# A SwiGLU layer as seven block products, and causal attention by pairs of heads, in a whole-model kernel

## The chip, the cores and the metric

The kernel runs on one core of a Trainium2 chip, as one launch that computes two transformer blocks. The metric is the device time in microseconds (us). The core has five engines with a queue each: TensorE (PE, matrix products; its weight loads are listed apart, as PEld), VectorE (DVE), ScalarE (ACT), GpSimd (POOL) and SyncE (SP, which issues most DMAs). Each engine works through its own queue in order, and an instruction starts when the results that it waits for are there.

## The reference, cut to what matters

The model has a first block (windowed attention and a spatial gate beside each other, then a mixture of experts) and a second block of two layers (a retention and state-space mixer in layer 0, a latent attention in layer 1), each layer followed by a SwiGLU feed-forward. All inputs are float32. The change touches two places.

The feed-forward of layer 1, on 512 tokens of 1024 features, with 2816 hidden features:

```python
def swiglu(h, w_gate, w_up, w_down):
    return (jax.nn.silu(h @ w_gate) * (h @ w_up)) @ w_down
...
h_lat = h_lat + m_lat[5] * swiglu(modulate(rms_norm(h_lat), m_lat[3], m_lat[4]),
                                  w_ffn_gate[i], w_ffn_up[i], w_ffn_down[i])
```

The first block's attention, 8 heads of 64 features on 512 tokens:

```python
DILATION_PATTERNS = ((128, 1), (512, 4), (2048, 16))
...
def dilated_mixture_attention(q, k, v):
    res = [dilated_window_attention(q, k, v, w, d) for (w, d) in DILATION_PATTERNS]
    m_all = jnp.stack([r[1] for r in res], 0)
    l_all = jnp.stack([r[2] for r in res], 0)
    o_all = jnp.stack([r[0] for r in res], 0)
    wts = l_all * jnp.exp(m_all - jnp.max(m_all, 0, keepdims=True))
    o = jnp.sum(wts[..., None] * o_all, 0) / jnp.sum(wts, 0)[..., None]
```

The three patterns weighted by their denominators are one causal softmax over all earlier keys, in which a key counts as often as patterns hold it. The kernel computes it so, with a table `amask` that is added to the scores.

## The kernel before, in words

The program is built by a scheduler that takes operations in the order in which the code gives them, with their tile pools, and writes out one queue per engine; within a queue nothing is reordered on the chip. A tile pool with a tag and `bufs=n` is a ring of n buffers: a new tile waits until the last reader of the one n tiles ago is done.

A float32 matrix product with full precision is three products of a shorter format: `split` (L238) makes of a tile a rounded part h (a cast on ACT, L239) and a rest l (a subtraction on DVE, L240), and `mm3` (L245) issues A_h B_h, A_h B_l and A_l B_h. Weights arrive by DMA in `wr` (a ring of 6 buffers of 128x1024), and their parts go to `wh` and `wl` (rings of 4).

The feed-forward of layer 1 is the class `FFN` with one sequence of 512 tokens; in this text it is the second feed-forward layer. Hidden features are taken in 11 chunks of 256, each of two blocks of 128 (`mi`). `gate_up(c)` makes for a block the gate product and the up product: 8 feature tiles x 3 matmuls of 512 columns each, into two PSUM tiles `gb`, 48 matmuls; then silu (ACT, L1490), the product with the up half (DVE, L1491) and the split of the result into `hidh` and `hidl`. Chunk 0 does it in halves of 256 columns (`cb`). `down(c)` multiplies the chunk's hidden features by two 128x512 tiles of down weights for each of four token tiles (`ob`, 48 matmuls of 512 columns, two PSUM banks "dn"), and DVE adds each `ob` to the accumulators `acc0` to `acc3` (L1534 for the first chunk, L1536 for the later). `run` gives out gate_up(c + 1) before down(c), for c up to 9; the scheduler then sets the 48 down products of chunks 0 to 8 between the gate products of the chunk two later, or next to it, as results come.

In the first block's attention a loop over 8 heads makes for each head four score products (one for each tile of 128 queries, against 128, 256, 384 or 512 keys; K = 64, so a head lies on rows 0 to 63 or 64 to 127), adds the mask and takes the maximum on DVE (L395, L396), the exponential on ACT, four reciprocals in one instruction, the scaling on DVE (L402), ten transposes on PE (`tpb`, L409), their copies, and for two heads together the value products (`pvb`). Between them `fill` sets products of the second block's conditioning (`adb`), FL[3] = 3 of them after each head.

## The time and profile before

| | before |
|---|---|
| device time, median of 3 runs | 2349.05 us (2348.92 to 2360.97) |
| the profiled execution | 2353.49 us, its span 2351.7 us |
| mean granted TensorE clock | 0.977 |
| PE busy | 2252.5 us, 96% |
| DVE, ACT, POOL busy | 61%, 34%, 19% |
| first block's attention | 86 to 156 us |
| feed-forward of layer 0 | 1005 to 1560 us |
| feed-forward of layer 1: chunk 0 | 1975 to 2001 us |
| feed-forward of layer 1: gate, up and down, chunks 1 on | 2001 to 2289 us, then the last down products |

Busy times are of one execution, taken by the profiler. They don't add up over engines, since engines work beside each other. A chain of waits is followed back from an instruction to what released it, so it shows which engine set the time at each moment; an engine with a high busy share that is not in the chain has time to spare. The granted clock is the share of TensorE's full clock that the chip gave it.

### The profile page before, as it was taken

Reading aid. Unit: us, or ns where it says so; the run is one execution under the profiler, and the core shown is the slowest. Engines: PE = TensorE matmul, PEld = TensorE weight load, DVE = VectorE, ACT = ScalarE, POOL = GpSimd, SP = SyncE. Lnnn points to the kernel's source line nnn. Section 1 sums busy time; section 2 is a strip of 40 time slices with the busy share of each in tenths; the row PEclk is TensorE's granted clock in tenths of the full one; section 3 lists DMA queues with packets and bytes.
Section 4 is the critical chain, followed back from the end, with each engine's and each line's share of the span. In section 5 each row is a group of like instructions: output and inputs, shape, how many; then the busy total and the mean of one; then the engine's idle time right before and its main releaser. Section 6 shows DMA issues by size and latency. Waiting matters only on the chain.

```text
span 2351.7 us, 30149 instructions
## 1 busy us (share of the span) xinstructions
PE 2252.5 (96%) x11748; PEld 1688.6 (72%) x11748; DVE 1423.6 (61%) x2341; ACT 794.9 (34%) x1382; POOL 442.9 (19%) x331
## 2 busy tenths in 40 slices
PE   9999999999979988899999999989999999999998
PEld 7667755534458756688888888877877668888876
DVE  8766743434475577776677753465568765444446
ACT  4344323222253243342211112134446545222222
POOL 0010310232250256410000000531022123000006
PEclk9999999999989997999999999999999999999999
DMA  8655498998853001344344331221100043332230
GB/s 297 217 183 202 182 373 332 371 389 336 310 197 99 30 28 54 125 152 135 122 139 135 126 108 55 65 97 62 60 1 1 1 147 107 106 99 92 87 106 39
DMA packets 99151, 338.91 MB, mean 144 GB/s; under 512 B 14373, under 2 KB 16293, under 8 KB 99002
## 3 DMA queue, kind: packets, MB, share of 16 engines
q1 hardware_dynamic: 94394, 324.33, 39.1%
q0 software_dynamic: 4608, 12.59, 1.5%
q8 instruction: 94, 1.54, 0.3%
q14 instruction: 55, 0.45, 0.1%
HBM read 323.21 MB, written 17.86 MB: 145 GB/s over the span
## 4 chain that ended last, share of the span: by engine, by line
PE 72%; DVE 8%; issue 3%; POOL 2%; ACT 2%; DMA 0%; POOLq 0%; SPq 0%; DVEq 0%; ACTq 0%
PE gb L243 22%; PE ob L243 14%; PE ga L243 10%; PE cb L243 6%; PE gu L243 5%; PE sc L243 3%; PE yb L243 3%; PE ptb L1808 2%; DVE wl L240 1%; POOL rs_r L290 1%; PE kb L243 1%; PE vb L243 1%; PE ntb L920 1%; PE ssd_x L243 1%; PE tpm L687 1%
## 5 line engine op out<-in xcount | busy, mean ns | idle before, releaser
L239 ACT CAST wh<-wr 128x1024 fp32r<-128x1024 f32 (+1 forms) x239 | 249.1, 1048 | 629.1 <-PE gb L243 274.9
L240 DVE TENSOR_TENSOR wl<-wr,wh 128x1024 fp32r<-128x1024 f32 (+1 forms) x235 | 309.2, 1323 | 216.4 <-ACT wh L239 211.8
L243 PE MATMUL gb<-fh,wh 128*128 128x512 f32 x672 | 264.0, 393 | 0.0
L243 PE MATMUL gb<-fh,wl 128*128 128x512 f32 x672 | 263.9, 393 | 0.0
L243 PE MATMUL gb<-fl,wh 128*128 128x512 f32 x672 | 263.7, 392 | 0.0
L243 PE MATMUL ob<-wh,hidh 128*128 128x512 f32 x440 | 173.9, 395 | 4.4 <-DVE gob L1529 3.0
L243 PE MATMUL ob<-wl,hidh 128*128 128x512 f32 x440 | 172.5, 392 | 0.0
L243 PE MATMUL ob<-wh,hidl 128*128 128x512 f32 x440 | 172.3, 392 | 0.0
L1536 DVE TENSOR_TENSOR acc<-acc,ob 128x512 f32<-128x512 f32 x160 | 108.3, 685 | 84.6 <-PE ob L243 84.6
L860 DVE SCALAR_TENSOR_TENSOR adacc<-wr,cond,adacc 128x512 f32<-128x512 f32 x224 | 152.9, 752 | 1.4 <-DMA wr<-in_w_ada 1.4
L243 PEld LDWEIGHTS gb<-fh,wl 128*128 128x128 f32 x672 | 126.2, 188 | 28.7
L243 PEld LDWEIGHTS gb<-fl,wh 128*128 128x128 f32 x672 | 126.2, 188 | 27.7
L243 PEld LDWEIGHTS gb<-fh,wh 128*128 128x128 f32 x672 | 126.2, 188 | 27.4
L243 PE MATMUL gu<-mw,xgT 128*64 128x512 f32 x512 | 124.3, 600 | 0.7 <-issue 0.7
L243 PE MATMUL cb<-fh,wh 128*128 128x256 f32 x416 | 118.0, 284 | 0.0
L243 PE MATMUL cb<-fl,wh 128*128 128x256 f32 x416 | 117.6, 283 | 0.0
L243 PE MATMUL cb<-fh,wl 128*128 128x256 f32 x416 | 117.0, 281 | 0.0
L1538 POOL TENSOR_TENSOR acc<-acc,gate 128x1024 f32<-128x1024 f32 x10 | 28.1, 2811 | 468.1 <-DVE acc L1536 468.1
L290 POOL TENSOR_TENSOR rs_r<-rs_v,mhalf 128x1 f32<-128x1 f32 (+1 forms) x54 | 46.4, 861 | 336.8 <-DVE rs_v L288 336.5
L243 PEld LDWEIGHTS ob<-wh,hidh 128*128 128x128 f32 x440 | 82.6, 188 | 24.8 <-DVE gob L1529 3.2
L1491 DVE TENSOR_TENSOR sg<-sg,gb 128x512 f32<-128x512 f32 x42 | 28.9, 688 | 112.3 <-PE gb L243 112.2
L243 PEld LDWEIGHTS ob<-wh,hidl 128*128 128x128 f32 x440 | 82.7, 188 | 18.3
(666 smaller groups left out, 4891.3 us busy)
## 6 DMA issues: line engine op xcount, KB each, us to landing
mw<-in_w_gu SPq DMA_DIRECT2D x128, 512.0 KB
wr<-in_w_ada SPq DMA_DIRECT2D x96, 512.0 KB
mw<-in_w_dn SPq DMA_DIRECT2D x64, 512.0 KB
wr<-in_w_fg SPq DMA_DIRECT2D x44, 512.0 KB
wr<-in_w_fu SPq DMA_DIRECT2D x44, 512.0 KB
wr<-in_w_fd SPq DMA_DIRECT2D x44, 512.0 KB
wr<-in_w_ret SPq DMA_DIRECT2D x28, 512.0 KB
wr<-in_w_in SPq DMA_DIRECT2D x19, 512.0 KB
```

The lines of the kernel that those rows point to most:

```text
L239: self.nc.scalar.copy(h, src)
L240: (eng or self.nc.vector).tensor_tensor(l, src, h.bitcast(F32), ALU.subtract)
L243: self.nc.tensor.matmul(out, lhsT, rhs, start=start, stop=stop, **kw)
L290: nc.gpsimd.tensor_tensor(r, v, self.mhalf[:, :n], ALU.pow)
L687: nc.tensor.transpose(bank[:, k, :], xg[:, (j * 4 + k) * P:(j * 4 + k + 1) * P], self.ident)
L860: V.scalar_tensor_tensor(acc[:, r], W[:, k], s, acc[:, r], op0=ALU.mult, op1=ALU.add)
L920: nc.tensor.transpose(bank[:, j, i * P:i * P + P], hp[i][:, (2 * kk + j) * P:(2 * kk + j + 1) * P], self.ident)
L1491: nc.vector.tensor_tensor(t, t, out[1], ALU.mult)
L1536: V.tensor_tensor(a[:, sl], a[:, sl], ob, ALU.add)
L1538: G.tensor_tensor(a, a, gate(tt), ALU.mult)
L1808: nc.tensor.transpose(bank[:, qt * P:qt * P + P], prs[h][qt][:, kt * P:kt * P + P], K.ident)
```

## The change

**Feed-forward of layer 1.** With `seven=True`, chunks 1 to 10 no longer compute the gate and the up half as two products. The activations (1024 features x 512 tokens) and the pair of weights are cut in 2 x 2 blocks (feature halves by token halves; gate and up by feature halves), and the 2 x 2 block product is formed by Winograd's variant of Strassen's scheme: seven products of blocks instead of eight, of sums of blocks, and sums of the seven. `sums` forms four sums of activation blocks once and splits them; `prep(m)` forms for each block of 128 hidden features four sums of weight blocks on POOL (L1510 to L1513) and splits gate, `sa`, `sb` and up; `seven_up(m)` issues the seven products (4 feature tiles x 3 matmuls x 256 columns each), two copies on ACT, five additions from PSUM on DVE, two additions on POOL (L1544, L1545), silu, and the product of the halves on DVE (L1549). `sa` and `sb` take places in the ring `wr`; `sah` and `sal` have rings of two in a new pool. The weights, the down products and the accumulators stay (the accumulator add is L1632 there).

**First block's attention.** The loop goes over four pairs of heads and the query tiles from the last to the first. The scores of the two heads of a pair are issued one behind the other, on rows 0 to 63 and rows 64 to 127, into banks of two tags; the softmax with its reciprocal is done for each head and query tile; transposes and value products of a pair are issued between the scores of the next. Fills are (2, 2, 1, 1) per pair.

```diff
-FL = (0, 1, 1, 3, 1)
+FL = (0, 1, 1, (2, 2, 1, 1), 1)
...
-        for h in range(8):
-            hp, b0 = h // 2, 64 * (h % 2)
...
-            for qt in range(NT):
-                n = (qt + 1) * P
-                sc = ps.tile([P, 512], F32, name="sc", tag="sc", bufs=2)
-                self.mm(sc[:, :n], qT[b0:b0 + 64, hp, qt * P:qt * P + P], kT[b0:b0 + 64, hp, :n], True, True)
...
-            V.reciprocal(ri, ls)
...
-            fill(FL[3])
+        room = self.res.rearrange("p t d -> p (t d)")[:, :2560].rearrange("p (i n) -> p i n", i=2)
+        def scores(p, qt):
+            n = (qt + 1) * P
+            sc = [ps.tile([P, 512], F32, name="sc", tag=tag, bufs=2) for tag in ("sc", "mm")]
+            for c in range(2):
+                r = slice(64 * c, 64 * c + 64)
+                self.mm(sc[c][:, :n], qT[r, p, qt * P:qt * P + P], kT[r, p, :n], True, True)
+            for c in range(2):
...
+                V.tensor_tensor(pv, sc[c][:, :n], amask[:, 512 - n:], ALU.add)
+                V.tensor_reduce(mx, pv, AX, ALU.max, negate=True)
+                S.activation(pv, pv, AF.Exp, bias=mx, accum_out=ls)
+                V.reciprocal(ls, ls)
+                V.tensor_scalar(pv, pv, ls, None, op0=ALU.mult)
...
+        for p in range(5):
+            for i in range(NT):
+                if p < 4:
+                    scores(p, NT - 1 - i)
+                    fill(FL[3][i])
+                if p and i:
+                    spread(p - 1, i - 1)
+                    if i > 1:
+                        values(p - 1, i - 2)
+            if p:
+                spread(p - 1, 3)
+                for jt in (2, 3):
+                    values(p - 1, jt)
...
+    def sums(self):
+        V, G = self.nc.vector, self.nc.gpsimd
+        (f11, f12), (f21, f22) = self.F
+        G.tensor_tensor(f11, f12, f11, ALU.subtract)
+        V.tensor_tensor(f12, f22, f12, ALU.subtract)
+        G.tensor_tensor(f22, f22, f11, ALU.subtract)
+        V.tensor_tensor(f21, f21, f22, ALU.subtract)
...
+        for n, t in (("t3", f12), ("t2", f22), ("t4", f21), ("t1", f11)):
...
+            self.K.split(t, h, l)
...
+    def prep(self, m):
...
+        g, u = (K.wraw(self.I[n][self.layer, m], (8, P)) for n in ("w_fg", "w_fu"))
+        sa, sb = K.w4("sa").rearrange("p (k c) -> p k c", c=P), K.w4("sb")[:, :512].rearrange("p (k c) -> p k c", c=P)
+        lo, hi = slice(0, 4), slice(4, 8)
+        G.tensor_tensor(sb, u[:, lo], u[:, hi], ALU.add)
+        G.tensor_tensor(sa[:, lo], sb, g[:, lo], ALU.subtract)
+        G.tensor_tensor(sa[:, hi], g[:, lo], u[:, lo], ALU.subtract)
+        G.tensor_tensor(u[:, lo], g[:, hi], sa[:, lo], ALU.subtract)
+        gs = K.wcut(g, (8, P))
+        sh, sl = (self.hpool.tile([P, 8, P], F32R, name=n, tag=n, bufs=2) for n in ("sah", "sal"))
+        K.split(sa, sh, sl)
+        ss = K.wcut(sb, (4, P))
+        us = K.wcut(u, (8, P))
...
+    def seven_up(self, m, hid, mi):
...
+        def product(a, t):
+            b = ps.tile([P, 512], F32, name="w" + a, tag="gu", bufs=6)[:, :w]
+            for k in range(4):
+                K.mm3(b, A[a](k), B[t](k), k == 0, k == 3)
+            return b
...
+        S.copy(c12, product("a11", "b11"))
+        V.tensor_tensor(c11, c12, product("a12", "b21"), ALU.add)
+        V.tensor_tensor(c12, c12, product("s2", "t2"), ALU.add)
+        V.tensor_tensor(c21, c12, product("s3", "t3"), ALU.add)
+        S.copy(m5, product("s1", "t1"))
+        self.prep(m + 1)
+        G.tensor_tensor(c12, c12, m5, ALU.add)
+        G.tensor_tensor(c22, c21, m5, ALU.add)
+        V.tensor_tensor(c12, c12, product("s4", "b22"), ALU.add)
+        V.tensor_tensor(c21, c21, product("a22", "t4"), ALU.add)
+        S.activation(t, t, AF.Silu)
+        V.tensor_tensor(t, t, v, ALU.mult)
+        K.split(t, hid[0][:, mi, :], hid[1][:, mi, :])
...
+        if self.seven and c:
+            for mi in range(2):
+                self.seven_up(2 * c + mi, hid, mi)
+            return hid
```

In the DVE queue of before, around the end of a chunk's second block, the two down-weight splits (`wl_17151` and `wl_17157`) stand in these rows, with the product of gate and up (L1491), the gate and up splits of the next block and the first accumulator add:

```order
L240 TENSOR_TENSOR wl_17151<-wr_17148,wh_17150 128x1024
L1491 TENSOR_TENSOR sg_17088<-sg_17088,gb_17039 128x512
L240 TENSOR_TENSOR wl_17157<-wr_17154,wh_17156 128x1024
L240 TENSOR_TENSOR hidl_17013<-sg_17088,hidh_17012 128x512
L240 TENSOR_TENSOR wl_17229<-wr_17226,wh_17228 128x1024
L1491 TENSOR_TENSOR sg_17143<-sg_17143,gb_17094 128x512
L240 TENSOR_TENSOR wl_17235<-wr_17232,wh_17234 128x1024
L240 TENSOR_TENSOR hidl_17013<-sg_17143,hidh_17012 128x512
L1536 TENSOR_TENSOR acc0_15917<-acc0_15917,ob_17160 128x512
L1536 TENSOR_TENSOR acc0_15917<-acc0_15917,ob_17168 128x512
```

The same place in the DVE queue of after; `wl_17988` and `wl_17994` are the down weights, L1541, L1546, L1547 and L1539 the sums out of PSUM, `sal` the rest of `sa`:

```order
L1541 TENSOR_TENSOR su_17853<-sg_17852,ws3_17897 128x256
L240 TENSOR_TENSOR wl_17948<-wr_17927,wh_17947 128x1024
L1546 TENSOR_TENSOR sg_17852<-sg_17852,ws4_17953 128x256
L1547 TENSOR_TENSOR su_17853<-su_17853,wa22_17967 128x256
L1549 TENSOR_TENSOR sg_17852<-sg_17852,su_17853 128x512
L240 TENSOR_TENSOR wl_17988<-wr_17985,wh_17987 128x1024
L240 TENSOR_TENSOR sal_18151<-sa_18140,sah_18150 128x1024
L240 TENSOR_TENSOR hidl_17718<-sg_17852,hidh_17717 128x512
L1632 TENSOR_TENSOR acc0_15977<-acc0_15977,ob_17997 128x512
L1539 TENSOR_TENSOR sg_18063<-sg_18063,wa12_18080 128x256
L240 TENSOR_TENSOR wl_17994<-wr_17991,wh_17993 128x1024
L1632 TENSOR_TENSOR acc0_15977<-acc0_15977,ob_18005 128x512
```

The first down weight's split now stands behind the product of the halves (L1549) and the second behind the first accumulator add, where both stood ahead of the block's last split before. The POOL queue of after has at this place, where that of before has nothing:

```order
L1510 TENSOR_TENSOR sb_18141<-wr_18138 128x512
L1544 TENSOR_TENSOR sg_17852<-sg_17852,m5_17854 128x256
L1545 TENSOR_TENSOR su_17853<-su_17853,m5_17854 128x256
L1511 TENSOR_TENSOR sa_18140<-sb_18141,wr_18136 128x512
L1512 TENSOR_TENSOR sa_18140<-wr_18136,wr_18138 128x512
L1513 TENSOR_TENSOR wr_18138<-wr_18136,sa_18140 128x512
L1510 TENSOR_TENSOR sb_18274<-wr_18271 128x512
```

The first weight sum of the next block (`sb`) stands ahead of the two sums of the current block, the other three (`sa` twice, `wr` for the changed up half) right behind them.

In the first block's attention the PE queue of before begins with one head's scores, with `adb` fills between:

```order
L243 MATMUL sc_835<-kT_781,qT_780 128x128
L243 MATMUL sc_840<-kT_781,qT_780 128x256
L243 MATMUL adb_328<-wr_890,cond_131 32x128
L243 MATMUL sc_845<-kT_781,qT_780 128x384
L243 MATMUL adb_328<-wr_890,cond_131 32x128 x2
L243 MATMUL sc_850<-kT_781,qT_780 128x512
L243 MATMUL adb_328<-wr_900,cond_131 32x128 x8
L243 MATMUL sc_913<-kT_781,qT_780 128x128
L243 MATMUL adb_328<-wr_969,cond_131 32x128 x5
L243 MATMUL sc_918<-kT_781,qT_780 128x256
L243 MATMUL sc_923<-kT_781,qT_780 128x384
```

In the queue of after, the second pair of heads has its scores of 512, 384 and 256 columns here, with fills and the first pair's transposes (`tpb`):

```order
L243 MATMUL sc_965<-kT_781,qT_780 128x512
L243 MATMUL adb_328<-wr_984,cond_131 32x128 x7
L243 MATMUL sc_966<-kT_781,qT_780 128x512
L243 MATMUL adb_328<-wr_984,cond_131 32x128
L243 MATMUL adb_328<-wr_994,cond_131 32x128 x8
L243 MATMUL sc_1004<-kT_781,qT_780 128x384
L243 MATMUL sc_1005<-kT_781,qT_780 128x384
L243 MATMUL sc_1067<-kT_781,qT_780 128x256
L415 MATMUL tpb_1054<-c_ident_63,pr_836 128x128 x4
L415 MATMUL tpb_1061<-c_ident_63,res_65 128x128 x4
L243 MATMUL sc_1068<-kT_781,qT_780 128x256
L415 MATMUL tpb_1095<-c_ident_63,pr_836 128x128 x3
```

The two scores of 384 columns are neighbours in the queue; those of 512 have fills between them, and those of 256 transposes.

## Rows read from the trace of the kernel before

**Rows 1.** The page, busy time of each engine.

```profile
PE 2252.5 (96%) x11748; PEld 1688.6 (72%) x11748; DVE 1423.6 (61%) x2341; ACT 794.9 (34%) x1382; POOL 442.9 (19%) x331
```

**Rows 2.** Windows: us, busy of each engine, granted clock, DMA share, GB/s.

```profile
2001.00:2289.00 288.00, 288.00 (x1259) 236.12 (x1259) 129.69 (x154) 75.44 (x91) 1.95 (x1) 1.00 0.30 97
...
85.00:156.00 71.00, 71.00 (x620) 39.64 (x620) 50.12 (x127) 38.87 (x100) 0.00 (x0) 1.00 0.59 200
```

**Rows 3.** Chain of waits, 2022.8 us on: start, us, engine, tile, line, count.

```profile
2022.79 2.80 PE ob L243 x12
2025.59 0.92 PE gb L243 x4
2026.51 8.39 PE ob L243 x36
2034.90 20.88 PE gb L243 x92
```

**Rows 4.** Chain of waits, chunk 0 of the second feed-forward layer.

```profile
1985.17 15.83 PE cb L243 x132
```

**Rows 5.** Groups, 2022.8 to 2088.8 us: shapes, count, busy us, mean ns, idle.

```profile
L240 DVE TENSOR_TENSOR wl<-wr,wh 128x1024 fp32r<-128x1024 f32 x12 | 14.7, 1224 | 14.2 <-ACT wh L239 13.7
...
L239 ACT CAST wh<-wr 128x1024 fp32r<-128x1024 f32 x13 | 13.7, 1053 | 53.0 <-PE gb L243 21.9 <-PE ob L243 19.4 <-issue 11.7
...
L1536 DVE TENSOR_TENSOR acc<-acc,ob 128x512 f32<-128x512 f32 x8 | 5.4, 684 | 4.0 <-PE ob L243 4.0
...
L240 DVE TENSOR_TENSOR hidl<-sg,hidh 128x512 fp32r<-128x512 f32 x4 | 2.7, 685 | 0.0
```

**Rows 6.** Timeline of 128x256 instructions: start, us, engine, line, operation, tiles.

```profile
1968.94 0.73 POOL L931 TENSOR_TENSOR fl<-ntf,fh 128x256 fp32r<-128x256 f32 x1 [4.42 <-ACT ntf L928]
...
1989.33 0.42 DVE L1491 TENSOR_TENSOR sg<-sg,cb 128x256 f32<-128x256 f32 x1 [1.85 <-ACT sg L1490]
```

**Rows 7.** Timeline, end of first feed-forward layer, POOL, DVE.

```profile
1548.35 5.08 POOL L1530 TENSOR_TENSOR res<-res,gob 128x512 f32<-128x512 f32 x4
...
1550.93 0.69 DVE L1529 TENSOR_TENSOR gob<-ob,gate 128x512 f32<-128x512 f32 x1 [0.67 <-POOL res L1530]
...
1553.01 0.96 DVE L1530 TENSOR_TENSOR res<-res,gob 128x512 f32<-128x512 f32 x1
```

**Rows 8.** Timeline around 161 us, POOL and DVE.

```profile
161.61 2.39 POOL L436 TENSOR_TENSOR wsp<-wsp,c_utri 128x1024 f32<-128x1024 f32 x1
...
161.69 2.87 DVE L447 TENSOR_TENSOR res<-res,ggb 128x512 f32<-128x512 f32 x1 [1.40 <-POOL res L446]
```

**Rows 9.** Timeline around 1974 us, DVE and POOL.

```profile
1974.20 2.35 DVE L240 TENSOR_TENSOR wl<-wr,wh 128x1024 fp32r<-128x1024 f32 x2
...
1974.35 2.80 POOL L931 TENSOR_TENSOR fl<-ntf,fh 128x256 fp32r<-128x256 f32 x1 [2.11 <-ACT ntf L928]
```

**Rows 10.** First block's attention: groups of matmuls, then timeline.

```profile
L243 PE MATMUL sc<-kT,qT 64*128 64x128 f32 (+3 forms) x64 | 22.8, 464 | 0.0
L243 PE MATMUL adb<-wr,cond 128*32 128x128 f32 x374 | 17.8, 279 | 0.0
L409 PE MATMUL tpb<-c_ident,pr 128*128 128x128 f32 x80 | 15.2, 292 | 0.0
L243 PE MATMUL pvb<-pt,v 128*64 128x256 f32 (+3 forms) x64 | 14.4, 447 | 0.0
...
90.52 0.48 PE L243 MATMUL sc<-kT,qT 64*128 64x128 f32 x2
...
93.33 1.12 PE L243 MATMUL sc<-kT,qT 64*128 64x512 f32 x2
...
94.73 0.33 PE L409 MATMUL tpb<-c_ident,pr 128*128 128x128 f32 x1
...
104.05 2.37 PE L243 MATMUL pvb<-pt,v 128*64 128x512 f32 x14
...
874.20 1.79 PE L243 MATMUL ret_s<-qT,kT 64*128 64x128 f32 x16
```

More of the change, by code (lines that the diff above doesn't have):

```diff
@@ L407, in block1, with spread @@
+        def spread(p, jt):
+            o, w = sum((NT - j) * P for j in range(jt)), (NT - jt) * P
+            for c in range(2):
+                if jt == 0:
+                    PTs[p, c] = p1.tile([P, 1280], F32, name="pt", tag="pt", bufs=3)
                 bank = ps.tile([P, 512], F32, name="tpb", tag="tp", bufs=2)
@@ L902, in rms, with norm_T @@
         return hn
-    def norm_T(self, hs, hn, nt, layer, which, row, outh, outl, pool, ps, tag, bufs):
+    def norm_T(self, hs, hn, nt, layer, which, row, outh, outl, pool, ps, tag, bufs, keep=None):
         nc = self.nc
@@ L925, in norm_T @@
                     nc.scalar.activation(h, bank[:, j, :], AF.Identity, scale=sc, bias=sh)
-                    f = pool.tile([P, 512], F32, name="ntf", tag="ntf", bufs=3)[:, :256]
+                    f = keep(k, pair) if keep else pool.tile([P, 512], F32, name="ntf", tag="ntf", bufs=3)[:, :256]
                     if j:
@@ L1418, with __init__ @@
 class FFN:
-    def __init__(self, K, layer, seqs, ps):
+    def __init__(self, K, layer, seqs, ps, seven=False):
+        self.seven = seven
+        self.preps = {}
         self.K, self.nc, self.I, self.layer, self.seqs, self.ps = K, K.nc, K.I, layer, seqs, ps
@@ L1435, in norm @@
         self.xs[si] = vh, vl, w
-        yield from self.K.norm_T(hs, hn, nt, self.layer, 1, row, vh, vl, npool, ps or self.ps, tag, bufs)
+        keep = None
+        if self.seven:
+            self.F = [[pool.tile([P, 4, 256], F32, name=f"xf{i}{j}", tag="xf", bufs=5) for j in range(2)] for i in range(2)]
+            keep = lambda k, pair: self.F[k // 4][pair][:, k % 4, :]
+        yield from self.K.norm_T(hs, hn, nt, self.layer, 1, row, vh, vl, npool, ps or self.ps, tag, bufs, keep)
     def open(self, pool):
-        self.pool = pool
+        self.pool = self.hpool = pool
         n = self.off[-1]
@@ new lines, in prep @@
+    def prep(self, m):
+        if m in self.preps or m >= DFF // P:
+            return
+        K, G = self.K, self.nc.gpsimd
+        g, u = (K.wraw(self.I[n][self.layer, m], (8, P)) for n in ("w_fg", "w_fu"))
[10 more added lines that the diff above has]
+        us = K.wcut(u, (8, P))
+        part = lambda t, o: lambda k: (t[0][:, o + k, :], t[1][:, o + k, :])
+        self.preps[m] = dict(a11=part(gs, 0), a12=part(gs, 4), s3=part((sh, sl), 4), s2=part((sh, sl), 0),
+                             s4=part(us, 0), a22=part(us, 4), s1=part(ss, 0))
@@ L1542, in run @@
         hid = self.gate_up(0)
+        if self.seven:
+            self.sums()
         for c in range(nch - 1):
@@ L2113, in body @@
         pg = opened("pg", k.pool("pg"))
-        f1 = FFN(k, 1, [(NT, 0)], psg)
+        f1 = FFN(k, 1, [(NT, 0)], psg, True)
         f1.open(pg)
```

69 lines of the change are left out of this document (35 added, 34 removed).

## The prediction

> **What bounds the kernel now.** I read the page first: TensorE (PE) is busy for 2252.5 of 2351.7 us, VectorE (DVE) for 61% of the span, ScalarE (ACT) for 34%, GpSimd (POOL) for 19% [rows 1]. The share is an average, so the windows come next, one on each place of the change. In the gate, up and down products of the second feed-forward layer (2001 to 2289 us) PE is busy in all 288.00 us, at a granted clock of 1.00, which is the 2.4 GHz level; DVE works 129.69 us there, and POOL does one instruction. In the first block's attention (85 to 156 us) PE is full too, DVE works 50.12 of 71 us and POOL nothing [rows 2]. The chain of waits through one period of the feed-forward (one chunk of 256 hidden columns) holds PE and nothing else: 12 down products, 4 gate products, 36 down products, 92 gate and up products, 2.80 + 0.92 + 8.39 + 20.88 = 32.99 us [rows 3]. So time can be won there only with fewer or cheaper products, and it is lost as soon as another engine delivers later than PE asks.
>
> **The seven products, PE.** Before, a block of 128 hidden columns took 48 matmuls of 512 columns (the chunk's 96 in [rows 3]); it now takes 7 x 4 x 3 = 84 of 256. A gate matmul of 512 takes 20.88/92 = 0.227 us [rows 3]; the nearest row for 256 is chunk 0 of the same layer, which the kernel before already does in halves: 15.83/132 = 0.120 us [rows 4]. So 84 x 0.120 - 48 x 0.227 = 10.08 - 10.90 = -0.82 us for a block, and -16.3 us for the 20 blocks of chunks 1 to 10. One eighth fewer columns give only 7.5%, since the step of a short matmul has a fixed part. By the ends: were 256 columns half of a 512 step (0.1135), 84 would cost 9.53 us and the 20 blocks win 27 us; that row's 0.120 has weight loads beside every matmul as the new products do, so I take it, and -20 (0.118, a rounding of it in 20 blocks) as the good end.
>
> **The seven products, the other engines.** Per block, with durations of [rows 5]: DVE had two splits of 128x1024 (1.22), one product (0.69) and one split (0.69), and now has three splits of 1024, one of 512, five sums out of PSUM of 128x256 (0.42 by [rows 6]), the product and its split: 3 x 1.22 + 0.69 + 5 x 0.42 + 2 x 0.69 = 7.8 us in place of 3.8. A chunk has two blocks, eight accumulator adds (0.68) and two splits of down weights: 15.6 + 5.5 + 2.4 = 23.5 us in a period of 168 x 0.120 + 48 x 0.2325 = 31.3 us on PE (0.2325 is 8.39/36). ACT has eight instructions per block and two casts per chunk, none over the 1.05 us of a cast of 1024: under 19 us in a period, which PE covers. POOL goes from nothing to four 128x512 sums (5.08/4 = 1.27 us each [rows 7]) and two of 128x256 (0.73 [rows 6]) per block, 13.2 us per period. Each engine alone fits below 31.3 us. The ring of six raw weights now also holds two sums per block, so weight transfers are issued later; the DMA engines are busy 0.30 of this stretch [rows 2], and I price that at nothing, up to 1 us per chunk if a landing is what PE waits for.
>
> They don't work alone. A DVE product of two SBUF operands, 0.69 us by itself, took 2.87 us when it started 0.08 us after a POOL instruction of 2.39 us: it stood until POOL was done [rows 8]. Beside the four POOL sums that ran from 1548.35 to 1553.43, a DVE instruction that reads PSUM took its normal 0.69 us, and one with both operands in SBUF 0.96 us, ending 0.5 us after POOL [rows 7]. It goes both ways: a POOL subtraction of 0.73 us took 2.80 us beside two DVE splits [rows 9]. All splits, the product of gate and up, and POOL's sums are of that kind; the PSUM sums and the accumulator adds aren't.
>
> That agrees with the Trainium skill, "SBUF — State Buffer", "Who interferes with whom": an exclusive lock, taken by whichever starts first and held for the whole instruction, between a DVE instruction with two SBUF inputs and a GpSimd instruction that reads SBUF. It speaks against this change, as nothing in the steady period of before used POOL: by it the stall worked out next is 3.2 us per chunk, and if both engines only went on side by side it would be 0.7. The 2.87 us agrees with it; the 0.96 us is a shorter wait than a whole POOL instruction would give.
>
> I walk one period by hand with the order of the changed kernel and these durations; t = 0 is the end of an odd block's last product. POOL has its two 256 sums (after the copy of m5, which ACT makes behind a weight cast) from -0.65 to 0.7, and then three 512 sums queued. The first holds 0.7 to 1.95. DVE's product of gate and up comes at 1.4, behind the silu, and waits to 1.9, ends 2.55. POOL's second holds 2.5 to 3.75. Next on DVE is the split of the first down weight: it waits to 3.7 and ends 4.85. PE asks for it at 2.62: after 12 gate products (1.44), one down product, which needs only the cast, and 8 more gate products comes the first down product that reads the split part. PE is in order, so it stands 2.3 us. POOL's third sum holds to 6.05, then DVE's split of sa to 7.15, the split of the hidden block 7.75, and the first accumulator add 8.35, where PE wanted its bank at 7.85: 0.5 to 0.6 more. The second down weight is split by 9.85, wanted at 9.6: 0.3 more. Together 3.2 us, in each of the 9 chunks whose down products are interleaved (0 to 8): +28.8 us. Behind the waiting splits stand the accumulator adds, and PE's two banks for down products wait for these. The same walk with DVE and POOL side by side leaves 0.7 us, since the split of the down weight stands behind the silu and the product in DVE's order either way: +6.3 over the 9 chunks. An upper end is an alternation over the whole period: 23.5 + 13.2 = 36.7 us against the 32.99 of before, which is +5.4 over PE's 31.3, 9 times +49.
>
> **The start.** The sums of activations and the first blocks' sums of weights are new work between the norm and chunk 1. Chunk 0 ends at 2001.0 on PE (1985.17 + 15.83, [rows 4]). From about 1987 DVE has two sums and four splits of 1024, the first block's four splits, the chunk's products and hidden splits: some 13 us; POOL has two 1024 sums (2.39 each) and seven 512 sums in that stretch: 14 us. In turn they need up to 27 us, side by side 14, and PE has 14 us of chunk 0 to cover them, then 10 us of block products that need only the first of them. I put +6.5 us, bounds 3 (side by side) and 10.
>
> **The attention.** It has 64 score matmul records (22.8 us), 374 fill products (17.8), 80 transposes (15.2), 64 value matmuls (14.4) [rows 10]. A score product of 512 columns (fp32, two records) takes 1.12 us by itself, one of 128 columns 0.48. Two heads on the two halves of the rows can share the array: the later stage with K = 64 does 16 records of 128 columns in 1.79 us, 0.11 each, where the two of 128 alone take 0.24 each [rows 10]. Of the 16 pairs only 9 stand back to back in the new order; 7 have a fill, a transpose or a value product between them. Half of 9/16 of 22.8 would be -6.4; I take -5.5, since short pairs also pay their start. The value products overlapped in pairs before (14 in 2.37 us); more of them are now split: +2.2. The first pair's softmax (two heads by four blocks on DVE, 32 reciprocals where 8 were) must end before the first transpose, which came at 94.73 us; I estimate 12.4 us from the first score, and fills that cover all but 1.8 us. Fills are 24 blocks as before. Sum -5.5 + 2.2 + 1.8 = -1.5, bounds -6 (all of the overlap, no idle) and +4 (none, idle 4). Elsewhere in the program a few instructions change places on every engine; I price that at nothing, 3 us to either side.
>
> **Sum.** -16.3 + 28.8 + 6.5 - 1.5 = +17.5 us on the profiled execution of 2353.49 us, which is 4.4 us over the median of the runs, 2349.05. So 2371 as a profile, **2366 us** as a median.
>
> **Rivals.**
> 1. Lock without loss: POOL's sums fall where DVE is in PSUM sums or idle, and PE stands 0.7 per chunk. -16.3 + 6.3 + 3 - 1.5 = -8.5: 2340 us; with 0.118 and the whole attention, 2329. For it: DVE has 7.8 us free per period; against: three POOL sums are queued just where the down weights are split. Chance 0.27.
> 2. Half: a stall of 2 us per chunk (one POOL sum less in the way, because after a stall of PE the splits come earlier relative to the products): -16.3 + 18 + 4 - 1.5 = +4: 2353 us. Chance 0.27.
> 3. DVE with POOL becomes the bound over the whole period: it decides when waiting in turn takes more than 31.3 us; DVE's 23.5 plus 13.2 is 36.7, less what DVE does meanwhile without the lock, 9.7 us of PSUM sums and accumulator adds. +5 per chunk in the worst case: -16.3 + 45 + 8 - 1.5 = +35: 2384 us. Against: four tenths of DVE's time are free of the lock. Chance 0.10.
> 4. The attention loses what it should win because split pairs step as single ones: +6 on any case; it lies inside the ranges.
> My forecast has 0.36.
>
> **Range and chances.** What a measurement here can tell from no change is about 0.5%, 11.7 us: faster is below 2337.3, slower above 2360.8. The forecast runs from 2356 to 2376 (stalls 2.1 to 4.3). Faster: two thirds of rival 1 and little else, 0.22. Slower: the forecast but for its low end, a fifth of rival 2, rival 3: 0.47. Same: 0.31. The range leaves out the good end of rival 1 and half of rival 3: 2334 to 2382.
>
> **What would show it.** In the profile of the changed kernel: products w... at 0.120 us each, 84 per block (else the first term). Idle of PE in front of down products, put down to DVE's split of a down weight, 2 to 3 us once per chunk, and DVE splits of 1024 that take 2 to 2.5 us beside a POOL sum (else the lock's term; with no such idle rival 1 holds). A busy share of DVE near 1.0 in the steady part would show rival 3. Idle of PE after 2001 us of 3 to 10 us tells the start; the scores' total, 17 us in place of 22.8, and idle before the first transpose the attention. The forecast is wrong if PE stays full in the steady part.

## The result, and the profile after

The changed kernel takes 2407.86 us (median of 4 runs, 2406.15 to 2411.25) where the kernel before takes 2351.64: ratio 1.0234, 95% interval 1.0201 to 1.0266. It is slower, as forecast, by three times what was forecast.

The page of the changed kernel, busy times and the granted clock in 40 slices:

```profile
PE 2263.3 (94%) x12468; PEld 1730.6 (72%) x12468; DVE 1535.2 (64%) x2511; ACT 840.7 (35%) x1466; POOL 603.4 (25%) x453
...
PEclk9999999999899987999999999999999999988988
```

PE has 720 records more than before [rows 1] and only 11 us more busy time; its share fell from 96 to 94%, and the clock is below 0.9 in three of the six slices of the second feed-forward layer, where it was 1.00 [rows 2]. The windows, with the columns of [rows 2], are chunk 0, and then one period each, from one chunk's first long run of down products to the next:

```profile
1975.00:2004.00 29.00, 23.43 (x177) 23.25 (x176) 18.66 (x27) 16.50 (x27) 13.25 (x9) 0.88 0.12 37
...
2109.00:2146.40 37.40, 34.19 (x216) 31.23 (x216) 25.70 (x33) 12.77 (x20) 15.89 (x13) 0.91 0.26 85
```

A period is 37.4 us where it was 32.99 [rows 3]; PE is idle for some 3 us of it and runs at a clock of 0.91. DVE with 25.7 us and POOL with 15.9 are far from full. PE's waits from 2035 to 2335 us (who waited for whom, us in total, times, longest):

```profile
PE ob L243 <- ACT wh L239: 17.3, 8, 2.9
PE ob L243 <- DVE wl L240: 7.9, 8, 1.2
```

Two waits per period, 2.2 and 1.0 us. The longer is one for ACT's cast of the first down weight, not for DVE's split of it. What leads to it stands in the timelines of SP's queue, POOL, DVE, ACT and PE, of one period:

```profile
2098.90 0.33 SPq L223 DMA_DIRECT2D wr<-in_w_fu  x1
...
2102.29 1.39 POOL L1510 TENSOR_TENSOR sb<-wr 128x512 f32<-128x512 f32 x1 [6.76 <-DMA wr<-in_w_fu]
2103.64 0.73 POOL L1544 TENSOR_TENSOR sg<-sg,m 128x256 f32<-128x256 f32 x1
...
2104.41 0.42 DVE L1546 TENSOR_TENSOR sg<-sg,ws 128x256 f32<-128x256 f32 x1 [1.88 <-POOL sg L1544]
...
2104.86 0.63 ACT L1548 ACTIVATE sg<-sg 128x512 f32<-128x512 f32 x1 [3.33 <-DVE sg L1546]
2105.40 1.03 ACT L239 CAST wh<-wr 128x1024 fp32r<-128x1024 f32 x1
...
2105.61 1.21 DVE L1549 TENSOR_TENSOR sg<-sg,su 128x512 f32<-128x512 f32 x1
...
2106.24 1.74 POOL L1512 TENSOR_TENSOR sa<-wr 128x512 f32<-128x512 f32 x1
2108.05 2.14 POOL L1513 TENSOR_TENSOR wr<-wr,sa 128x512 f32<-128x512 f32 x1
...
2106.75 2.31 DVE L240 TENSOR_TENSOR wl<-wr,wh 128x1024 fp32r<-128x1024 f32 x1
...
2106.48 0.50 PE L243 MATMUL ob<-wh,hidh 128*128 128x512 f32 x1 [2.03 <-ACT wh L239]
...
2109.11 0.80 PE L243 MATMUL ob<-wl,hidh 128*128 128x512 f32 x1 [0.93 <-DVE wl L240]
```

Read it downwards. The next block's up weights are asked for at 2098.90, the moment the ring of raw weights has a place (DVE's split that held it ends at 2098.88), and POOL's first weight sum starts at 2102.29, behind the transfer. Behind that sum, in POOL's queue, stand the two additions of the fifth product of the block that is being finished; DVE's L1546 waits for the first, silu for that, and the cast of the down weight stands behind silu on ACT. PE stands 2.03 us. DVE's product and split then run beside POOL's next sums and take 1.21 and 2.31 us, where the block before took 0.69 and 1.22; POOL's sums take 1.74 and 2.14 us for 1.27. That is the lock of the prediction, and PE stands 0.93 us for the split. And after the long standing a product of 256 columns takes 0.213 us from start to start in place of 0.119, and one of 512 takes 0.427 in place of 0.233: half speed, the 1.2 GHz level. The window over this stretch has a granted clock of 0.50:

```profile
2107.48:2114.31 6.83, 5.90 (x23) 5.12 (x23) 6.33 (x6) 2.88 (x4) 2.64 (x2) 0.50 0.44 154
```

A stretch of 6.83 us like this follows the wait for the cast in every period.

At the start POOL's first weight sums (L1510 to L1513, 1971.39 to 1979.39 us) come ahead of a small instruction (L290) that the last norm needs; PE stands 5.57 us (timelines of POOL, DVE, PE):

```profile
1971.39 2.21 POOL L1510 TENSOR_TENSOR sb<-wr 128x512 f32<-128x512 f32 x1 [1.49 <-DVE wl L240]
...
1979.35 1.53 POOL L290 TENSOR_TENSOR rs_r<-rs_v,mhalf 128x1 f32<-128x1 f32 x1
...
1980.91 1.88 DVE L918 TENSOR_SCALAR acc<-res,rs_r 128x512 f32<-128x512 f32 x2 [0.44 <-POOL rs_r L290]
...
1982.54 1.51 PE L938 MATMUL ntb<-c_ident,acc 128*128 128x128 f32 x6 [5.57 <-DVE acc L918]
```

The attention gained. Two heads' scores of 512 columns that are neighbours take as long as one head's (first row), against a pair that is not (second row):

```profile
88.08 1.13 PE L243 MATMUL sc<-kT,qT 64*128 64x512 f32 x4
...
96.09 1.12 PE L243 MATMUL sc<-kT,qT 64*128 64x512 f32 x2
```

From the first score to the last value product it is 63.6 us in place of 68.0. By steps from start to start the scores take 3.3 us less and the value products 2.4 more; fills and transposes take 3.1 less, PE stands 0.8 us, and the rest is that fewer products of the next stage fall into this stretch.

Set against the kernel before at the same marks, the profiled executions differ so: -4.1 us up to chunk 0, +14.2 from there to the first down product, +35.7 in the next eight periods (299.5 against 263.8), +8.3 in the last one, +0.2 behind it; 54.3 in all.

### The profile page after: what moved, and what is told of

Its sections match the earlier page's. It is cut to its first block, busy times and chain, and to the rows that moved or that the text cites. A ratio compares the mean times of both kernels' runs of the same rounds, so it can differ in the third digit from the quotient of the medians.

```text
span 2406.0 us, 32156 instructions
## 1 busy us (share of the span) xinstructions
PE 2263.3 (94%) x12468; PEld 1730.6 (72%) x12468; DVE 1535.2 (64%) x2511; ACT 840.7 (35%) x1466; POOL 603.4 (25%) x453
## 5 line engine op out<-in xcount | busy, mean ns | idle before, releaser
L240 DVE TENSOR_TENSOR wl<-wr,wh 128x1024 fp32r<-128x1024 f32 (+1 forms) x235 | 316.4, 1353 | 152.2 <-ACT wh L239 149.5
L1632 DVE TENSOR_TENSOR acc<-acc,ob 128x512 f32<-128x512 f32 x160 | 108.3, 685 | 95.8 <-PE ob L243 95.8
L243 PE MATMUL gb<-fh,wh 128*128 128x512 f32 x352 | 139.3, 396 | 0.0
L243 PE MATMUL gb<-fh,wl 128*128 128x512 f32 x352 | 139.2, 396 | 0.0
L243 PE MATMUL gb<-fl,wh 128*128 128x512 f32 x352 | 139.2, 395 | 0.0
L290 POOL TENSOR_TENSOR rs_r<-rs_v,mhalf 128x1 f32<-128x1 f32 (+1 forms) x54 | 47.4, 882 | 328.0 <-DVE rs_v L288 327.8
L243 PEld LDWEIGHTS ob<-wl,hidh 128*128 128x128 f32 x440 | 85.0, 193 | 28.1 <-DVE wl L240 10.4
L243 PEld LDWEIGHTS gu<-mw,xgT 128*64 128x64 f32 x512 | 37.3, 138 | 72.9 <-issue 67.9
L243 PE MATMUL ga<-wl,ah 128*128 128x512 f32 x208 | 84.1, 407 | 3.4 <-DVE wl L240 3.0
L243 PE MATMUL ga<-wh,ah 128*128 128x512 f32 x208 | 85.2, 411 | 1.2 <-ACT cva L1085 1.2
```

Of the source, the lines that this page charges most:

```text
L240: (eng or self.nc.vector).tensor_tensor(l, src, h.bitcast(F32), ALU.subtract)
L243: self.nc.tensor.matmul(out, lhsT, rhs, start=start, stop=stop, **kw)
L290: nc.gpsimd.tensor_tensor(r, v, self.mhalf[:, :n], ALU.pow)
L1632: V.tensor_tensor(a[:, sl], a[:, sl], ob, ALU.add)
```

## The experiments

Three theories stood against each other. Chain: POOL waits in line for a transfer, and silu and the down weight's cast wait behind it. Lock: the port to SBUF that DVE and POOL share and hold in turn, my forecast's term. Width: products of 256 columns bring the clock down by themselves. The period is read from PE's timeline, from one chunk's first down product to the next one's; idle is the sum of PE's listed waits from 2060 to 2260 us, with the granted clock of that stretch:

| kernel | period, us | idle in 200 us | clock | ratio to before (95%) |
|---|---|---|---|---|
| before | 32.97 | 0 | 1.00 | 1 |
| after | 37.4 | 18.5 | 0.91 | 1.0234 (1.0201 to 1.0266) |
| attention alone | 33.0 | 0 | 1.00 | 0.999 (0.997 to 1.0009) |
| fifth product added by DVE | 34.6 | 12.1 | 1.00 | 1.0107 (1.0075 to 1.0139) |
| no weight sums | 32.5 | 4.2 | 1.00 | 0.9997 (0.998 to 1.0014) |
| seven products from chunk 2 | 36.9 | 14.9 | 0.93 | 1.0147 (1.0115 to 1.0179) |
| filler products | 37.6 | 6.7 | 1.00 | 1.024 (1.0194 to 1.0285) |
| no weight sums, DVE adds | 31.7 | 0 | 1.00 | one run |
| the same, port held by POOL | 32.3 | 2.1 | 1.00 | one run |
| from chunk 2, DVE adds | 34.6 | 10.2 | 1.00 | 1.0055 (1.0037 to 1.0073) |
| up weights first | 35.1 | 14.1 | 0.98 | 1.0146 (1.0113 to 1.0178) |
| from chunk 2, DVE adds, up first | 33.45 | 5.2 | 1.00 | 1.0018 (0.9999 to 1.0036) |
| the same, own ring for a sum | 33.07 | 2.4 | 1.00 | 1.0006 (0.9986 to 1.0027) |
| the same, last chunk as before | 33.1 | 2.2 | 1.00 | 0.997 (0.9952 to 0.9988) |

**The attention alone.** The kernel before with the attention's part of the change.

> The kernel before with the attention by pairs of heads and nothing else. In the changed kernel's trace everything up to chunk 0 of the second feed-forward layer begins 4.1 us earlier than before, of which 4.4 us come between the first score and the last value product. If the attention part is what that shows, this kernel takes 2347 us where before takes 2351, ratio 0.998; the feed-forward keeps its period of 33.0 us at a granted clock of 1.00. Rival: the reshuffled order of the whole program is what moved the 4.1 us, then the ratio is 1.000 or over.

The stretch from scores to values gains the same 4.4 us in its trace; the ratio is near what was expected (0.998), but its interval reaches past 1, so the whole can't be told from no change. The 4.1 us by which the changed kernel reached chunk 0 earlier say little: this kernel and the five below that are the same as it up to there begin chunk 0 anywhere from 1964.4 to 1971.3 us.

**The fifth product added by DVE.**

```diff
-        S.copy(m5, product("s1", "t1"))
-        self.prep(m + 1)
-        G.tensor_tensor(c12, c12, m5, ALU.add)
-        G.tensor_tensor(c22, c21, m5, ALU.add)
+        m5 = product("s1", "t1")
+        V.tensor_tensor(c12, c12, m5, ALU.add)
+        V.tensor_tensor(c22, c21, m5, ALU.add)
+        self.prep(m + 1)
```

> The changed kernel, with the two additions of the fifth product taken from POOL and its copy from ACT: VectorE adds it straight out of PSUM, so that silu, and the cast of the down weight behind silu in ACT's queue, no longer wait behind POOL's first weight sum, which waits for a weight transfer (2098.90 to 2102.16 us). Chain theory: the 2.03 us of idle in front of the first down product goes, 1 us of it stays for the split of the down weight beside POOL's sums, the clock stays near 1.00, and the period falls from 37.4 to 33 us or less: 2365 to 2375 us in place of 2408. Lock theory (the port that VectorE and POOL share is the cause, as I forecast): POOL still holds it with the four weight sums, so 3 us of idle stay and the period stays above 36.5: 2400 us or more. Width theory (products of 256 columns bring the clock down by themselves): granted clock of 0.91 as before this edit, period 35: 2386 us.

It took 32 us off (2375.85 against 2407.86), 22 of them in the eight periods and 9 in the last chunk; the clock is 1.00 with the same 256-column products, and the period 34.6. The lock and the width theory both fall as the main cause, though the edit also takes 2.9 of POOL's some 13 us per period away; the chain's number for the period was 1.6 us too low, because a second place in line was left. ACT's and PE's timelines of this kernel:

```profile
2133.94 1.05 ACT L239 CAST sah<-sa 128x1024 fp32r<-128x1024 f32 x1 [3.23 <-POOL sa L1512]
2134.89 0.61 ACT L239 CAST hidh<-sg 128x512 fp32r<-128x512 f32 x1
2135.41 0.37 ACT L1537 COPY sg<-wa 128x256 f32<-128x256 f32 x1
2135.68 1.04 ACT L239 CAST wh<-wr 128x1024 fp32r<-128x1024 f32 x1
```

```profile
2132.81 0.50 PE L243 MATMUL ob<-wl,hidh 128*128 128x512 f32 x1 [0.61 <-DVE wl L240]
2136.78 0.50 PE L243 MATMUL ob<-wh,hidh 128*128 128x512 f32 x1 [1.00 <-ACT wh L239]
2137.61 0.50 PE L243 MATMUL ob<-wh,hidh 128*128 128x512 f32 x1 [0.34 <-DVE acc L1631]
```

The second down weight's cast stands on ACT behind the cast of `sa`, which waits for POOL. Waits of 0.61, 1.00 and 0.34 us did not bring the clock down here; in the changed kernel the one of 2.03 us did. The cheaper edit that would have told the place in line from the work itself, POOL's two additions kept but given out ahead of `prep(m + 1)`, was not run.

**The weight sums left out, with POOL and with DVE adding the fifth product.** `sa, sb = g, u[:, lo]` takes the place of the four sums.

> The changed kernel without the four sums of weight blocks of each block of 128 columns: the products that take them read raw halves of gate and up in their place; splits, products, sums of products and activation sums stay. POOL has no instruction that waits for a weight transfer or holds the port for long, and the ring of raw weights has two tiles per block as in the kernel before. Chain and lock theory: no idle on PE in the steady period, 31.3 to 32 us at a granted clock of 1.00, so 9 x 5.5 to 6 us less, and some of the start: 2345 to 2355 us. Width theory: the clock stays at 0.91 and the period above 34: 2380 us.

> The weight sums left out as in the run without them, and the fifth product added by VectorE: POOL does nothing in the steady period. The base for the next run. Chain and lock theory: idle under 0.7 us, clock 1.00, period 32.0 to 32.6 us; VectorE's two more additions of 0.42 us per block are covered.

In both the clock is 1.00, as chain and lock said and width did not. The first is in its range by time (2351) but not by period: 32.5 us, since PE still stands 0.7 us in each for the down weight's cast, which stays behind silu on ACT; no idle was expected. The second, at 31.7 us, is below its 32.0. It is what seven products cost when nothing is late: with 48 down products of 0.2325 that leaves 20.5 us for 168, 0.122 each. (From start to start they step by 0.119; the rest is some 0.1 us at each of five changes to and from down products.) The best that this scheme had to give is 1.27 us per chunk, 0.5% of the program over ten chunks. The first also lost 6.83 us in the last chunk, where POOL's additions of the fifth product stand in line behind its scaling of the accumulators, and the changed kernel loses the same there (last row). POOL's and DVE's timelines of the first in the last chunk, and PE's of the changed kernel:

```profile
2307.96 2.34 POOL L1632 TENSOR_TENSOR res<-res,acc 128x1024 f32<-128x1024 f32 x1
2310.26 0.72 POOL L1541 TENSOR_TENSOR sg<-sg,m 128x256 f32<-128x256 f32 x1
...
2311.01 0.42 DVE L1543 TENSOR_TENSOR sg<-sg,ws 128x256 f32<-128x256 f32 x1 [10.13 <-POOL sg L1541]
...
2368.39 0.58 PE L243 MATMUL ws<-xht,wh 128*128 128x256 f32 x1 [6.84 <-DVE sg L1546]
```

DVE stands 10.13 us for an addition of 0.72 us that waited only for its turn.

**Filler products.** In `down`, ahead of the first down product of chunks 1 to 8:

```diff
+            if self.seven and tt == n == 0 and 0 < c < DFF // 256 - 2:
+                for _ in range(21):
+                    K.mm(ob, hid[0][:, 0, :P], hid[0][:, 1, :512], True, True)
```

> The changed kernel with 21 wasted products of 512 columns ahead of the first down product of chunks 1 to 8, into the same bank, overwritten by the real ones. They need nothing that is late. In the changed kernel PE stands 2.03 and 0.93 us there and then runs at half speed from 2107.55 to 2114.7 us. If the slow clock comes from the standing (idle theory), the wasted 21 x 0.233 = 4.9 us fill the idle, the granted clock goes back to about 1.00, and a period is 31.8 + 4.9 + 0.3 = 37.0 us: as long as without them, 2400 to 2410 us. If the clock falls for another reason (width theory, or the place in the program), idle is filled but the clock stays near 0.91 and a period gets at least 2 us longer, 39.5 to 42: 2425 to 2450 us.

PE's timeline of this kernel, and the window from 2060 to 2260 us:

```profile
2107.93 4.94 PE L243 MATMUL ob<-hidh 128*128 128x512 f32 x21
2112.71 0.40 PE L243 MATMUL ob<-wh,hidh 128*128 128x512 f32 x1
2114.41 0.50 PE L243 MATMUL ob<-wl,hidh 128*128 128x512 f32 x1 [1.31 <-DVE wl L240]
2114.75 0.40 PE L243 MATMUL ob<-wh,hidl 128*128 128x512 f32 x1
```

```profile
2060.00:2260.00 200.00, 193.27 (x1276) 175.44 (x1275) 137.28 (x172) 69.90 (x100) 82.84 (x64) 1.00 0.27 89
```

A period with 4.9 us of wasted products is as long as one without (37.6 against 37.4), because the clock stays at its upper level: the slow stretch came from the standing, and the wait for the cast and the slow clock together were worth about the 4.9 us. So the fillers gave the clock back and won no time. The Trainium skill, "TensorE: Matmul & The Clock Gate", "HAM oscillation — how this bites in real kernels", tells of a loop that falls back to the lower clock in each pass because it waits for data. The changed kernel's trace agrees, with 6.83 us at the lower level in each period.

The length of a wait doesn't settle the clock by itself. In one period of this run PE stands 2.05 us for the split, and the clock stays at 1.00 (PE's row, and a window over it):

```profile
2190.60 0.50 PE L243 MATMUL ob<-wl,hidh 128*128 128x512 f32 x1 [2.05 <-DVE wl L240]
...
2186.00:2198.00 12.00, 9.95 (x59) 8.43 (x58) 9.22 (x9) 4.56 (x6) 6.42 (x5) 1.00 0.27 87
```

**The port alone.** To the kernel without weight sums, four POOL sums per block that nobody waits for:

```diff
+        d, r = (self.last if mi == 0 else hid[0][:, 0, :]), K.res
+        for q in range(4):
+            G.tensor_tensor(r[:, 0, :512], d.bitcast(F32), r[:, 1, :512], ALU.add)
```

> The same with four POOL sums of 128x512 per block put back that nobody waits for: they read the hidden block just cast and a residual tile, write the residual tile (so the output is not the model's), and wait for no transfer. They hold the port as the weight sums did, at the same place of the period. Lock theory (my forecast's walk): VectorE's product and the split of the first down weight wait for them, 2 to 3 us of idle in front of down products, period 34 to 37 us. Chain theory: what the weight sums cost was mostly waiting in line for a transfer, the port alone costs under 1 us of idle: period 32.3 to 33.2 us.

DVE's and POOL's timelines of this kernel:

```profile
2125.18 1.65 DVE L240 TENSOR_TENSOR wl<-wr,wh 128x1024 fp32r<-128x1024 f32 x1
2126.76 0.41 DVE L1545 TENSOR_TENSOR sg<-sg,ws 128x256 f32<-128x256 f32 x1
2127.09 0.41 DVE L1546 TENSOR_TENSOR su<-su,wa 128x256 f32<-128x256 f32 x1
2127.42 1.65 DVE L240 TENSOR_TENSOR wl<-wr,wh 128x1024 fp32r<-128x1024 f32 x1
```

```profile
2130.46 6.90 POOL L1544 TENSOR_TENSOR res<-hidh,res 128x512 f32<-128x512 f32 x4 [2.48 <-ACT hidh L239]
```

The port is held: a split takes 1.65 us for 1.22, a POOL sum 1.73 for 1.27, and a PSUM sum its normal 0.41, in which POOL goes on. It costs 0.6 us per period, not 3. These sums start at the cast of a hidden block, somewhat later than the real ones, so the 0.6 stands for the load on the port, not for the worst place. The one run takes 18.3 us more than its base all the same: 7.2 lie before chunk 0, where the two kernels are the same, 4.7 in the eight periods and 6.4 behind them, where PE stands 4.34 us in one place for DVE.

**The start.** `if self.seven and c > 1`, with `sums` called behind chunk 1.

> The changed kernel with chunk 1 computed as before too, and the activation sums formed behind it. In the changed kernel POOL's first weight sums stand in its queue ahead of the small instruction (L290) that the last norm needs, and PE waits 5.57 us for it. Chain theory: the start loses its two waits (5.57 and 1.65 us) and their slow clock, about 12 us, against 1.6 us for two blocks at the old price: 2398 us in place of 2408, the steady period still 37.4. Rival: the start is bound by the sums of activations themselves (some 14 us of work on VectorE and POOL), which come one chunk later with as much to do: within 4 us of 2408.

The start's 14 us went whole: its first down product stands where the kernel before would have it (the marks from chunk 0 on agree within 0.3 us). The time is 2387.44 where 2398 was expected, since the period, expected unchanged, fell to 36.9.

**The transfer.** The up weights are fetched first: `u, g = (... for n in ("w_fu", "w_fg"))`.

> The changed kernel with one edit: a block's up weights are fetched before its gate weights. POOL's first weight sum needs the up weights alone, which in the changed kernel land at 2102.16 us, 2.3 us behind the gate weights; everything behind that sum in POOL's queue, and silu and the down weight's cast behind it, would start up to 2.3 us earlier. Chain theory: the 2.03 us of idle in front of the first down product shrinks to under 0.5, the split's 0.93 stays or grows to 1.5 since POOL's sums still stand beside it, the clock comes back to 0.97 or more, period 33 to 35 us: 2365 to 2385 us. Lock theory: POOL holds the port as long as before, at a moment 2 us earlier; idle of 2.5 us or more and a period above 36: 2395 us or more.

One swap of two transfers took 18.5 us off, with all of POOL's work left as it was. The clock came back to 0.98 and the period to 35.1; the time, 2389, is a little over its range. Idle stayed at 14.1 us in 200, more than expected, now half for the cast and half for the split: POOL's addition takes 1.72 us beside a DVE split in place of 0.73, so against PE's products it ends 0.9 us earlier and not 2.3. Waits of the same size left the clock up in one period and brought it down for 3.4 us in another (timelines of POOL and PE, windows over the two periods):

```profile
2130.24 1.72 POOL L1544 TENSOR_TENSOR sg<-sg,m 128x256 f32<-128x256 f32 x1
...
2134.07 0.50 PE L243 MATMUL ob<-wh,hidh 128*128 128x512 f32 x1 [1.11 <-ACT wh L239]
2136.72 0.50 PE L243 MATMUL ob<-wl,hidh 128*128 128x512 f32 x1 [1.20 <-DVE wl L240]
...
2168.94 0.50 PE L243 MATMUL ob<-wh,hidh 128*128 128x512 f32 x1 [1.12 <-ACT wh L239]
2171.59 0.57 PE L243 MATMUL ob<-wl,hidh 128*128 128x512 f32 x1 [1.20 <-DVE wl L240]
...
2130.00:2140.00 10.00, 7.68 (x53) 6.66 (x52) 8.96 (x8) 4.50 (x7) 7.74 (x6) 1.00 0.18 59
2166.00:2176.00 10.00, 7.68 (x44) 6.77 (x43) 8.64 (x10) 4.45 (x6) 6.60 (x5) 0.83 0.28 81
```

**Repairs together.**

> Both repairs in one: seven products from chunk 2 on, and the fifth product added by VectorE. If their savings are separate places of the program they add up: the first saved 20 us of 2408 and the second 32, so 2355 to 2362 us, period 34.6. If both took away the same wait: 2370 or more. Even so the period stays above the 33.0 of the kernel before, so that the kernel with the attention alone (2349) isn't beaten.

> Seven products from chunk 2 on, the fifth product added by VectorE, and up weights first. The kernel with the first two took 2365 us at a period of 34.58, with 0.60 us of idle for the down weight's split beside POOL's sums, 1.00 for the second down weight's cast, which stands on ACT behind the cast of a weight sum, and 0.34 for the accumulator. If the sums start 2 us earlier all three shrink: period 32.5 to 33.5, 2346 to 2356 us. If another wait (the ring of raw weights) takes over, the period stays above 34 and the time at 2362 or more.

> The same, and one of the two sums of weight blocks (sb) taken out of the ring of raw weights into its own ring of two, for which the cast part of the other sum (sah) gives up one of its two buffers. Ring theory: weight transfers are issued earlier, since a chunk now takes 8 places of the ring and not 10; no wait in front of POOL's sums, period 31.7 to 32.5 us, and 2340 to 2347 us, faster than the kernel before. Rival: the single buffer of sah holds ACT up until PE has done the products of the block before, and the period is 33.5 or more: 2355 us or more.

The savings add up to parity, and no further. The three runs take 2365, 2360 and 2358 us, each 3 to 11 us over its range, and in the session of the last two the kernel before itself takes 2356; the ratios are what compares. In the second, where the transfer is no longer late and POOL's additions are gone, the lock is seen at its real place: DVE's product and split take 0.93 and 2.23 us beside POOL's sums, and PE stands 0.8 us per period for the split, at a clock of 1.00. In the third, with idle nearly gone (2.4 us in 200), the period is 33.07, over the 31.7 without sums and the 32.97 of the old scheme. PE's listed waits explain 0.4 of these 1.4 us. By steps from start to start all of it stands at down products: what goes beyond 0.119 and 0.2325 us a step adds up to 1.95 us in one period (2143.53 to 2176.60) and to 0.57 in one without sums. The own ring took out 0.4 us; whether earlier transfers or the single buffer set the rest is open. In the last chunk of this third kernel the port shows at its worst (POOL, DVE and PE timelines):

```profile
2305.03 3.35 POOL L1633 TENSOR_TENSOR acc<-acc,gate 128x1024 f32<-128x1024 f32 x1
...
2306.07 2.86 DVE L1548 TENSOR_TENSOR sg<-sg,su 128x512 f32<-128x512 f32 x1
...
2315.49 0.77 PE L243 MATMUL ob<-wh,hidh 128*128 128x512 f32 x1 [4.51 <-DVE sg L1539]
```

**The last chunk as before.** `1 < c < DFF // 256 - 1`.

> The last kernel with chunk 10 computed as before, so that seven products are left in chunks 2 to 9. In the last kernel's trace VectorE's splits and products of chunk 10 (2296 to 2315 us) take 2.8 us each beside POOL's scaling of the accumulators (128x1024, 2.4 us each), and PE stands 1.64 and 4.51 us for two of them. Lock theory, for this place: the idle goes, PE works through to its last down products as in the kernel before, 6 to 8 us less against 1.3 us for two blocks at the old price: 5 to 6 us under the last kernel, ratio 0.998 to 0.9985 to before, about what the attention alone gives. Rival: the end is set by POOL's own chain of scalings and the last additions whatever PE does, and the time stays within 2 us of the last kernel.

0.997 (0.9952 to 0.9988): faster than the kernel before by 0.3%, and 5.6 us less than the last kernel in the profile (2341.0 against 2346.6), as expected. This version beats both kernels; by the ratios, how much of it is the attention's 0.999 can't be told apart. The traces tell more: from the first product of chunk 0 to the end it is 376.4 us before, 376.8 with the attention alone, 382.2 in the last kernel and 373.7 here, so some 3 us of the gain lie in the feed-forward, in one execution of each.

## Why the prediction was wrong

The sign was right, the size not: +17.5 us forecast for the profiled execution, +54.3 found, outside the range. The step that failed is the walk through one period: it had a standing PE go on at full clock, and it let POOL's sums start without waiting for a transfer. Of the 36.8 us that the forecast fell short, the slow clock is about 22, the start 8, the last chunk 4 and dearer products 3 to 4, against 3 that came back before chunk 0; these don't add up exactly, as the clock's share is an estimate.

- The products: 0.120 us was taken, 0.122 found; 1.63 us per chunk forecast, 1.27 found. The price of a step was right (0.119); the changes between block products and down products, 0.57 us per period, had no term. The sum's only other value, -20 for ten chunks, lay on the wrong side of the -12.7 found.
- The standing of PE: 3.2 us per chunk forecast, 3.2 found (2.2 and 1.0). The size was right by luck and the reason mostly wrong. The walk let POOL's sums start as soon as their operands were ready and priced late weight transfers at nothing, "up to 1 us per chunk if a landing is what PE waits for". That step failed: the landing is what POOL waits for, and POOL's queue, not PE's, hands the wait on through silu to ACT's cast. With t = 0 at 2102.86 us, the end of the odd block's last product in the period shown, POOL's additions ran from 0.8 to 2.2, not from -0.65 to 0.7: the next block's first weight sum stood ahead of them, from -0.6 to 0.8. The walk also took the cast as done ("one down product, which needs only the cast"), though it stands behind silu: PE wanted it at 1.6 and had it at 3.6. Without weight sums 0.7 us of this wait stay, so some 1.3 are the transfer's (an estimate). The lock was there, about as long as walked (product 1.21 us, split 2.31), but the walk gave it 2.5 of its 3.2 us; it costs 0.6 by itself, 0.8 where nothing else is late, and the 0.9 to 1.0 us of the split's wait in the full kernel. The 0.8 to 0.9 us forecast for a bank and for the second down weight did not come.
- The clock: the forecast read 1.00 in [rows 2] and carried it over to a kernel that stands 3 us per period. No term was made of it, and none of the rivals had it. Of the 37.4 us, 31.7 are products and 3.2 idle; the remaining 2.5 are the slow stretch, 22 us over nine chunks (an estimate by difference). With it the forecast would have been some 40, still under what was found.
- The start: +6.5 forecast (3 to 10), 14.2 found. The sums of activations were priced, but not that the weight sums would stand ahead of the norm's own POOL instruction, and the slow clock after that wait (0.88).
- The last chunk: no term; 3.8 us beyond another period. The accumulators' scaling on POOL, in the kernel before hidden behind gate products that need no POOL, now has the additions of the fifth product in line behind it; PE stands 6.84 us there (6.83 in the no-sums run), and with the additions on DVE this wait is gone.
- The attention: -1.5 forecast, -4.4 between its first and last product; inside the bounds, but not by the terms of the sum. The scores gave 3.3 us and not 5.5 (their busy total is 19.5 us, where the forecast named 17); the value products cost 2.4 (2.2 forecast) and idle 0.8 (1.8); most of the rest came from shorter steps of fills and transposes, which had no term.
- The rivals: the first, without loss, is what the run without sums and with DVE's additions shows, and the run with the own ring comes near its idle with POOL's weight sums in place (0.4 us per period), though not near its time, at a period of 33.07. The second, with 2 us per chunk, was too low. The third was not it: DVE is busy 25.7 of 37.4 us. The fourth lies inside the attention's 4.4 us.
- Slips that change nothing: 8.39/36 is 0.233 and not 0.2325, and POOL's sums add up to 13.1 us and not 13.2.

## What to carry to other kernels

When work moves to an idle engine, look first at what its queue waits for: a late transfer at its head holds up everything behind it, and through that engines that look unrelated. Price a new standing of PE with the slow clock behind it, here 2.5 us on top of 3.2. Filler products bring the clock back, but here they were as long as what they saved; removing the wait is what won time. A scheme that saves one product in eight by halving the width gave 3.9% of the period (1.27 of 32.97 us) at best, so its side work has to be free.

## What the runs showed of the hardware

In the changed kernel a wait of 2.03 us or more in an else full PE was followed, in each of its nine periods, by 6.83 us at the lower clock, which began no later than 1.5 us after PE had started again. The length of the wait alone doesn't decide it: one of 2.05 us in the filler run left the clock at 1.00, and two waits of 1.1 and 1.2 us close together brought it down in some periods of one run and not in others. Three waits of 0.34 to 1.00 us within 6 us did not bring it down. What decides between equal waits, no run here shows. Wasted products of 4.9 us in place of the wait kept the clock at 1.00 and cost nothing.

DVE instructions with two SBUF operands and POOL sums beside them stretch each other: a DVE split took 2.31 us for 1.22 and POOL's sums 1.74 and 2.14 us for 1.27, while sums out of PSUM kept their 0.41 us.
